# Four pairs by seven products, tiles at multiples of 64 bytes, and later transposes of the first hidden blocks in a four-layer float32 encoder

## The chip, the core and the metric

The kernel runs on one core of a Trainium2 chip. The metric is device time in microseconds (us) for one execution of the whole program. The engines are TensorE (PE, matmuls; its loads of the stationary operand are shown as PEld), VectorE (DVE), ScalarE (ACT), GpSimd (POOL) and SyncE (SP), which issues most DMAs. In the profile an operand name is a tile's name, and L229 is line 229 of the kernel.

## The reference, cut to what matters

The program computes four layers of an encoder on x of 256 rows and 1024 columns in float32. Each layer has a token mixer (chunked attention with a relative bias, gated linear attention, differential attention, and chunked attention again), a layer norm, a SwiGLU feed-forward with 2816 hidden columns, and a second layer norm:

```python
def swiglu(x, w_gate_up, w_down):
    g, u = jnp.split(x @ w_gate_up, 2, axis=-1)
    return (jax.nn.silu(g) * u) @ w_down

    for i in range(DEPTH):          # 4 layers
        y = mixer_i(h, ...)         # 0, 3: chunk band attention; 1: GLA; 2: differential attention
        h = layer_norm(DN_ALPHA * h + y, ln1_g[i], ln1_b[i])
        h = layer_norm(DN_ALPHA * h + swiglu(h, ffn_w_gate_up[i], ffn_w_down[i]), ln2_g[i], ln2_b[i])
```

## The kernel before

**Products.** Every float32 operand of a large product is split into a high part, rounded to the type fp32r, and a low part, the rest. A product is then three matmuls: high by high, low by high, high by low. `w_tiles` loads a pair of k-tiles of weights into `raw` (SP issues the DMA), casts the high part `wh` on ACT (L130) and subtracts the low part `wl` on DVE (L131). Two forms of product read these tiles. `run_rows` (L208 to L210) has activations as the stationary operand (`xT`, or `slab` in the output projections) and weights of 512 columns as the moving one. `run_cols` (L229, L230) has weights as the stationary operand and the activations as the moving one, 512 columns (both parts) and 256 columns (the high part): one pair of matmuls for each k-tile, eight pairs for each of the four blocks of a chunk, each block in one of four `mm` banks.

**The feed-forward** (`ffn`) runs over 11 chunks of 256 hidden columns, which are the 11 pairs of k-tiles of the down-projection. Chunks 0 and 1 go by rows: `row_done` makes the Silu on ACT (L932) and the product with the other half on DVE (L934), and `turn_hidden` transposes the result on PE (L943). Chunks 2 to 10 go by columns: `col_done` copies a block out of its bank on ACT (L968) and adds on DVE (L969). The hidden values are kept in `plain`, split into high and low.

**Seven products.** A pair in `SEVEN` is treated as a 2 by 2 product of blocks, which `seven_products` makes with 7 block products and not 8. Its hidden blocks go to `hid`; `combine` makes four sums of blocks on POOL (L916 to L919), and five steps later `split` makes the high parts on ACT (L924) and the low parts on DVE (L925), into `seven`. Its weights are loaded by `load`, which also makes three differences on DVE (L1015, into `tt` and back into `raw`) and then splits seven blocks and not four (`halves`: ACT L143, DVE L144). Each product of the down-projection is the three matmuls L1027 to L1029. After the last pair in `SEVEN`, `gather` adds the groups of products to the layer's sum on DVE. The loads of a chunk are written into the order one chunk ahead of its products; the tiles come from two rings, `raw` with 24 KB and `split` with 64 KB in each partition, in the pool `wp`.

**Order.** The code's order is the engines' order, except where a step is put off: `defer(n, f)` runs `f` after `n` steps of `tick`, one step for three matmuls of `run_rows`, for two pairs of `run_cols`, or for one product of the down-projection. `D_HIDDEN` is the number for `turn_hidden`, `D_COMBO` that for `split`.

**Addresses.** The pools lie one behind the other in each partition: `const` (`ident`, `powt`), `wp` (both rings), `act` (`h`, `xT`, the working tiles `k1`, small tiles), then the pool of the stage (`slab`, `k2`, `k3`, `plain`, `hid`, `seven`, `tt`, `gb`). A tile's size is rounded up to 32 bytes. `powt` holds 4 bytes and takes 32, so that in the built program all large tiles of `wp` and `act` start 32 bytes past a multiple of 64. The tiles of every stage start at a multiple of 64.

Of the kernel before, what the change touches and what calls it, by code (L numbers as in the profile page):

```python
# [9 lines left out]
F32 = mybir.dt.float32  # L10
# [5 lines left out]
P = 128  # L16
# [12 lines left out]

D_SCORES, D_TURN, D_TURN_DIFF, D_VALUES, D_VALUES_DIFF, D_OUT = 4, 7, 6, 3, 2, 6  # L30
D_GATE2, D_GATE3, D_STATE, D_READ, D_GLA_OUT = 3, 8, 2, 4, (6, 5)
D_NORM, D_HIDDEN, D_COMBO = 8, 4, 5
WARM = 24

SEVEN = (0, 3, 6)


@with_exitstack  # L40
def trunk_kernel(
# [27 lines left out]
    nc = tc.nc  # L69

    const = ctx.enter_context(tc.tile_pool(name="const", bufs=1))
# [3 lines left out]
    act = ctx.enter_context(tc.tile_pool(name="act", bufs=1))  # L75
# [18 lines left out]
    def st(shape, dtype, tag, bufs):  # L94
        return stage[-1].tile(shape, dtype, tag=tag, bufs=bufs, name=nm(tag))
# [18 lines left out]

    ident = const.tile([P, P], F32, tag="ident", name="ident")
    make_identity(nc, ident)
    powt = const.tile([P, 1], F32, tag="powt", name="powt")
    nc.gpsimd.memset(powt, -0.5)


    def w_tiles(chunk, s, fine=False):
# [17 lines left out]
    def halves(w, n):  # L139

        wh = split_ring.tile([P, n, 512], F32R, name=nm("wh"))
        wl = split_ring.tile([P, n, 512], F32R, name=nm("wl"))
        nc.scalar.copy(out=wh, in_=w)  # L143
        nc.vector.tensor_tensor(out=wl, in0=w, in1=wh.bitcast(F32), op=ALU.subtract)  # L144
        return [(wh[:, k, :], wl[:, k, :]) for k in range(n)]
# [95 lines left out]
    def put(dst, ks, cs, val):  # L241

        h = dst[:, ks, cs]
        nc.scalar.copy(out=h, in_=val)
        nc.vector.tensor_tensor(
            out=dst[:, ks, slice(256 + cs.start, 256 + cs.stop)],
            in0=val,
            in1=h.bitcast(F32),
            op=ALU.subtract,
        )  # L250
# [639 lines left out]
    def ffn(xT, layer, norm):  # L890
# [8 lines left out]
        n_pairs = FFN // 256  # L899
        rest = [c for c in range(n_pairs) if c not in SEVEN]  # L900
        plain = st([P, 2 * len(rest), 4 * P], F32R, "plain", 1)
# [20 lines left out]
        def split(c, f):  # L922
            x = seven[c] = st([P, 2, 7, P], F32R, "seven", len(SEVEN))
            nc.scalar.copy(out=x[:, 0], in_=f[:, 0:7, :])  # L924
            nc.vector.tensor_tensor(  # L925
                out=x[:, 1], in0=f[:, 0:7, :], in1=x[:, 0].bitcast(F32), op=ALU.subtract
            )
# [11 lines left out]
        def turn_hidden(c, t, hd):  # L939
            b = bank()  # L940
            for k in range(2):
                ks = slice(k * P, (k + 1) * P)
                nc.tensor.transpose(b[:, ks], hd[:, ks], ident)  # L943
            if c not in SEVEN:
                put(
# [17 lines left out]
        def col_done(c):  # L963
            g = {}

            def done(blk, b):
# [8 lines left out]
                gg = g.pop(k)  # L975
                if c not in SEVEN:
                    nc.vector.tensor_tensor(out=lo, in0=lo, in1=gg, op=ALU.mult)
# [26 lines left out]
        def load(c):  # L1004
            raw = raw_ring.tile([P, 4, 512], F32, name=nm("raw"))
            nc.sync.dma_start(raw, w_down[layer, c].rearrange("p (k n) -> p k n", k=4))
            if c not in SEVEN:
                parts[c] = halves(raw[:, 0:2], 2) + halves(raw[:, 2:4], 2)
# [39 lines left out]
        def seven_products(c):  # L1048
            for i, (a, b) in FORMS.items():
# [4 lines left out]
                    parts[c][b],  # L1054
                    c == SEVEN[-1] and i not in where,
                )
# [75 lines left out]
    for i in range(depth):  # L1132
# [18 lines left out]
        in_stage(ffn, norm1.xT, i, norm2)  # L1151
        xT = norm2.xT


def _layouts(inputs):

# [81 lines left out]
```

## Time and profile before

| | us |
|---|---|
| median of 3 runs | 1226.15 |
| lowest and highest run | 1224.26, 1227.82 |
| the profiled execution | 1226.83 |
| its span, first to last instruction | 1224.9 |
| PE busy | 1199.9 (98%) |
| DVE busy | 899.6 (73%) |
| ACT busy | 680.6 (56%) |
| POOL busy | 147.1 (12%) |

The profile is of one execution. A row of the timeline has a start, a duration, the engine, the line and the operation with its tiles, and in brackets how long the engine idled before it and what ended that. A matmul's printed duration overlaps with the next one's; the distance between two starts is what the queue pays. The granted clock of PE is at the upper of its two levels (1.2 and 2.4 GHz) all along.

### The profile page before, as it was taken

To read this page: it belongs to the slowest core of one execution; us is meant where nothing else is said; L and a number is where in the kernel's file an instruction comes from. 1 tells how busy PE (TensorE), PEld (TensorE's weight loads), DVE (VectorE), ACT (ScalarE), POOL (GpSimd) and SP (SyncE) were. 2 spreads that over 40 slices of the span, in tenths; PEclk is the share of its full clock that TensorE was granted. 3 is DMA by queue.
4 is the path that set the end of the run, shared out by engine and by line. 5 is a ranking of instruction groups with operands and counts; after the bars stand their busy time and mean duration, and the time that the engine had idled before them with its cause. 6 is when DMAs were issued, how large, how long until landed. Compare 5 with 4: busy or idle time off the path is not lost.

```text
span 1224.9 us, 17125 instructions
## 1 busy us (share of the span) xinstructions
PE 1199.9 (98%) x6212; PEld 990.0 (81%) x6212; DVE 899.6 (73%) x1490; ACT 680.6 (56%) x1185; POOL 147.1 (12%) x268
## 2 busy tenths in 40 slices
PE   8999999999999999999999999999999999999996
PEld 7888788888677878888887777888888888788885
DVE  6688766787656767677867786677786888676875
ACT  6566565653564455655446656566544774565550
POOL 1210101000211110110022211010002200101000
PEclk9999999999999999999999999999999999999999
DMA  9654645555474455556564355555656544655541
GB/s 362 213 181 125 213 157 194 190 194 202 144 230 132 139 188 197 179 181 227 194 211 153 127 162 171 202 190 176 218 189 232 188 139 147 198 171 199 189 172 35
DMA packets 56692, 223.88 MB, mean 183 GB/s; under 512 B 6816, under 2 KB 7328, under 8 KB 50976
## 3 DMA queue, kind: packets, MB, share of 16 engines
q1 hardware_dynamic: 51264, 206.59, 50.1%
q0 software_dynamic: 4768, 15.15, 3.9%
q10 hardware_dynamic: 576, 1.05, 0.3%
q8 instruction: 49, 0.80, 0.3%
q14 instruction: 35, 0.29, 0.1%
HBM read 221.71 MB, written 1.05 MB: 182 GB/s over the span
## 4 chain that ended last, share of the span: by engine, by line
PE 89%; POOL 3%; DVE 2%; DMA 2%; ACT 2%; issue 2%; POOLq 0%; DVEq 0%; ACTq 0%
PE mm L229 28%; PE mm L230 14%; PE mm L208 7%; PE mm L209 7%; PE mm L210 7%; PE tp L1027 5%; PE tp L1029 5%; PE tp L1028 5%; PE tp L468 2%; PE tp L257 1%; PE mm L1027 1%; PE mm L1028 1%; PE mm L1029 1%; PE tp L537 1%; DMA k<-in_c_bias_dram 1%
## 5 line engine op out<-in xcount | busy, mean ns | idle before, releaser
L229 PE MATMUL mm<-xT,wh 128*128 128x512 f32 x1568 | 559.3, 400 | 0.0
L230 PE MATMUL mm<-xT,wl 128*128 128x256 f32 x1568 | 441.4, 281 | 0.0
L131 DVE TENSOR_TENSOR wl<-raw,wh 128x1024 fp32r<-128x1024 f32 (+1 forms) x306 | 369.4, 1216 | 63.9 <-ACT wh L130 61.6
L130 ACT CAST wh<-raw 128x1024 fp32r<-128x1024 f32 (+1 forms) x306 | 314.0, 1045 | 112.6 <-PE mm L209 58.9
L229 PEld LDWEIGHTS mm<-xT,wh 128*128 128x128 f32 x1568 | 294.8, 188 | 74.3 <-issue 4.6
L230 PEld LDWEIGHTS mm<-xT,wl 128*128 128x128 f32 x1568 | 296.5, 189 | 0.7 <-issue 0.3
L144 DVE TENSOR_TENSOR wl<-raw,wh 128x1024 fp32r<-128x1024 f32 (+1 forms) x88 | 105.0, 1220 | 22.9 <-PE tp L1029 11.8
L208 PE MATMUL mm<-wh,xT 128*128 128x512 f32 x304 | 120.1, 398 | 1.6 <-ACT wh L130 1.3
L210 PE MATMUL mm<-wl,xT 128*128 128x512 f32 x304 | 119.4, 393 | 0.6 <-DVE wl L131 0.5
L209 PE MATMUL mm<-wh,xT 128*128 128x512 f32 x304 | 119.5, 394 | 0.0
L143 ACT CAST wh<-raw 128x1024 fp32r<-128x1024 f32 (+2 forms) x88 | 90.4, 1050 | 43.3 <-PE tp L1027 22.6
L969 DVE TENSOR_TENSOR k<-mm,k 128x256 f32<-128x256 f32 x144 | 60.5, 420 | 60.5 <-ACT k L968 60.5
L1027 PE MATMUL tp<-wl,plain 128*128 128x512 f32 x256 | 102.0, 398 | 0.0
L1028 PE MATMUL tp<-wh,plain 128*128 128x512 f32 x256 | 101.5, 396 | 0.0
L1029 PE MATMUL tp<-wh,plain 128*128 128x512 f32 x256 | 101.4, 396 | 0.0
L968 ACT COPY k<-mm 128x256 f32<-128x256 f32 x144 | 53.4, 370 | 62.2 <-PE mm L230 61.9
L208 PEld LDWEIGHTS mm<-wh,xT 128*128 128x128 f32 x304 | 56.9, 188 | 15.9 <-ACT wh L130 2.3
L209 PEld LDWEIGHTS mm<-wh,xT 128*128 128x128 f32 x304 | 57.1, 188 | 13.4 <-issue 1.2
L210 PEld LDWEIGHTS mm<-wl,xT 128*128 128x128 f32 x304 | 57.1, 188 | 13.3 <-DVE wl L131 1.8
L1029 PEld LDWEIGHTS tp<-wh,plain 128*128 128x128 f32 x256 | 48.2, 188 | 11.8
L282 POOL TENSOR_SCALAR sm<-mv 128x1 f32<-128x1 f32 x16 | 11.9, 746 | 380.6 <-DVE mv L346 380.6
L1028 PEld LDWEIGHTS tp<-wh,plain 128*128 128x128 f32 x256 | 48.2, 188 | 11.5
(190 smaller groups left out, 1478.4 us busy)
## 6 DMA issues: line engine op xcount, KB each, us to landing
raw<-in_w_gu_dram SPq DMA_DIRECT2D x176, 512.0 KB, 4.3
raw<-in_w_down_dram SPq DMA_DIRECT2D x44, 1024.0 KB, 5.0
raw<-in_a_qkv_dram SPq DMA_DIRECT2D x46, 512.0 KB, 5.3
raw<-in_b_in_dram SPq DMA_DIRECT2D x24, 512.0 KB, 4.3
raw<-in_c_qkv_dram SPq DMA_DIRECT2D x24, 512.0 KB, 4.4
raw<-in_a_o_dram SPq DMA_DIRECT2D x16, 512.0 KB, 3.8
k<-in_a_bias_dram POOLq DMA_DIRECT2D x16, 256.0 KB, 4.7
raw<-in_b_o_dram SPq DMA_DIRECT2D x8, 512.0 KB, 4.0
```

Source lines behind the costliest of these rows:

```text
L130: nc.scalar.copy(out=wh[:, k, :], in_=raw[:, k, :])
L131: nc.vector.tensor_tensor(out=wl[:, k, :], in0=raw[:, k, :], in1=wh[:, k, :].bitcast(F32), op=ALU.subtract,)
L143: nc.scalar.copy(out=wh, in_=w)
L144: nc.vector.tensor_tensor(out=wl, in0=w, in1=wh.bitcast(F32), op=ALU.subtract)
L208: nc.tensor.matmul(b, xh, wh, start=first, stop=False)
L209: nc.tensor.matmul(b, xl, wh, start=False, stop=False)
L210: nc.tensor.matmul(b, xh, wl, start=False, stop=last)
L229: nc.tensor.matmul(b, wh[:, cs], xk, start=kt == 0, stop=False)
L230: nc.tensor.matmul(b[:, :256], wl[:, cs], xk[:, :256], start=False, stop=kt == NKT - 1)
L1027: nc.tensor.matmul(o, xh, wl, start=start, stop=False)
L1028: nc.tensor.matmul(o, xh, wh, start=False, stop=False)
L1029: nc.tensor.matmul(o, xl, wh, start=False, stop=stop)
```

## The change

Three numbers change, and two tiles. `SEVEN` has pairs 0, 2, 4 and 6 in place of 0, 3 and 6, so that `plain` has 14 rows and not 16, `seven` has four buffers and not three, and one plain pair lies between two pairs by seven. `D_HIDDEN` goes from 4 to 10 steps. `powt` becomes the first column of a tile of 32 columns (128 bytes), and a tile of 32 bytes is added at the end of `act`; in the built program all large tiles then start at a multiple of 64 bytes.

```diff
-D_NORM, D_HIDDEN, D_COMBO = 8, 4, 5
+D_NORM, D_HIDDEN, D_COMBO = 8, 10, 5
-SEVEN = (0, 3, 6)
+SEVEN = (0, 2, 4, 6)
-    powt = const.tile([P, 1], F32, tag="powt", name="powt")
-    nc.gpsimd.memset(powt, -0.5)
+    pad = const.tile([P, 32], F32, tag="powt", name="powt")
+    nc.gpsimd.memset(pad, -0.5)
+    powt = pad[:, 0:1]
...
         in_stage(ffn, norm1.xT, i, norm2)
         xT = norm2.xT
+    act.tile([P, 8], F32, tag="pad", bufs=1, name="pad")
```

In the changed file lines after L118 stand two lines lower: L932 is L934 there, L943 is L945, L1015 is L1017.

ScalarE, first layer, where the row products of chunks 0 and 1 end and the column products begin. `hid_1441` and `hid_1466` are pair 0's blocks, `k_341` and `k_339` are the Silu of chunk 1's second half. Before:

```order
L130 CAST wh_1673<-raw_1672 128x1024
L959 COPY hid_1441<-tp_1518 128x128
L960 COPY hid_1441<-tp_1518 128x128
L130 CAST wh_1679<-raw_1678 128x1024
L924 CAST seven_1546<-hid_1441 128x896
L932 ACTIVATE k_341_1542<-mm_1508 128x256
L130 CAST wh_1685<-raw_1684 128x1024
L244 CAST plain_1348<-tp_1586 128x2x128
L968 COPY k_359_1595<-mm_1573 128x256
```

Now:

```order
L132 CAST wh_1686<-raw_1685 128x1024
L934 ACTIVATE k_339_1533<-mm_1503 128x256
L961 COPY hid_1466<-tp_1566 128x128
L962 COPY hid_1466<-tp_1566 128x128
L926 CAST seven_1600<-hid_1466 128x896
L970 COPY k_357_1587<-mm_1561 128x256
L973 ACTIVATE k_357_1587<-k_357_1587 128x256
L970 COPY k_360_1611<-mm_1591 128x256
L246 CAST plain_1348<-tp_1621 128x2x128
```

The Silu moved ahead of pair 0's copies and cast; behind the cast there are now the copies of the first column blocks.

TensorE at the same place: the transposes of chunk 1's second half (`k_342` before, `k_340` now) among the column products of chunk 2. Before, in the first block:

```order
L230 MATMUL mm_1573<-xT_1276,wl_1563 128x256
L943 MATMUL tp_1586<-ident,k_342_1544 128x128 x2
L229 MATMUL mm_1573<-xT_1276,wh_1568 128x512
L230 MATMUL mm_1573<-xT_1276,wl_1569 128x256
L229 MATMUL mm_1573<-xT_1276,wh_1568 128x512
```

Now, in the third block:

```order
L231 MATMUL mm_1616<-xT_1276,wh_1538 128x512
L232 MATMUL mm_1616<-xT_1276,wl_1539 128x256
L945 MATMUL tp_1621<-ident,k_340_1535 128x128 x2
L231 MATMUL mm_1616<-xT_1276,wh_1544 128x512
L232 MATMUL mm_1616<-xT_1276,wl_1545 128x256
```

They moved from behind 12 column matmuls to behind 36.

VectorE, first layer, where the last column chunks end and the loads of the down-projection begin; `raw_2600` and `raw_2604` are pair 1, `raw_2638` and `raw_2642` pair 2. Before:

```order
L245 TENSOR_TENSOR plain_1348<-k_513_2458,plain_1348 128x256
L969 TENSOR_TENSOR k_530_2529<-mm_2512,k_530_2529 128x256
L977 TENSOR_TENSOR k_530_2529<-k_530_2529,k_528_2508 128x256
L245 TENSOR_TENSOR plain_1348<-k_530_2529,plain_1348 128x256
L969 TENSOR_TENSOR k_532_2552<-mm_2535,k_532_2552 128x256
L144 TENSOR_TENSOR wl_2603<-raw_2600,wh_2602 128x1024
L144 TENSOR_TENSOR wl_2607<-raw_2600,wh_2606 128x1024
L144 TENSOR_TENSOR wl_2641<-raw_2638,wh_2640 128x1024
```

Now:

```order
L1017 TENSOR_TENSOR tt_2644<-raw_2642 128x1024
L247 TENSOR_TENSOR plain_1348<-k_516_2462,plain_1348 128x256
L971 TENSOR_TENSOR k_533_2533<-mm_2516,k_533_2533 128x256
L1017 TENSOR_TENSOR tt_2644<-tt_2644,raw_2642 128x512
L979 TENSOR_TENSOR k_533_2533<-k_533_2533,k_531_2512 128x256
L1017 TENSOR_TENSOR raw_2642<-raw_2642,tt_2644 128x512
L247 TENSOR_TENSOR plain_1348<-k_533_2533,plain_1348 128x256
L971 TENSOR_TENSOR k_535_2556<-mm_2539,k_535_2556 128x256
L146 TENSOR_TENSOR wl_2607<-raw_2604,wh_2606 128x1024
L146 TENSOR_TENSOR wl_2611<-raw_2604,wh_2610 128x1024
L146 TENSOR_TENSOR wl_2646<-raw_2642,wh_2645 128x512
L146 TENSOR_TENSOR wl_2652<-tt_2644,wh_2651 128x1536
```

Pair 2, now one by seven, has its three differences between the last sums of the column chunks, ahead of pair 1's subtractions.

## Rows read from the trace of the kernel before

**Rows 1.** The page: busy time of each engine, granted clock, chain by engine.
```profile
PE 1199.9 (98%) x6212; PEld 990.0 (81%) x6212; DVE 899.6 (73%) x1490; ACT 680.6 (56%) x1185; POOL 147.1 (12%) x268
...
PEclk9999999999999999999999999999999999999999
...
PE 89%; POOL 3%; DVE 2%; DMA 2%; ACT 2%; issue 2%; POOLq 0%; DVEq 0%; ACTq 0%
```

**Rows 2.** PE's waits: who waited for whom, total us, times, longest us.
```profile
PE tp L943 <- DVE k L934: 6.1, 4, 1.6
PE tp L624 <- DVE k L611: 1.5, 2, 0.8
```

**Rows 3.** Timeline at one of the four waits (start, duration, engine, operation, idle before).
```profile
146.42 0.46 POOL L919 TENSOR_TENSOR hid<-hid 128x128 f32<-128x128 f32 x1
146.91 0.94 ACT L924 CAST seven<-hid 128x896 fp32r<-128x896 f32 x1 [2.40 <-POOL hid L919]
147.76 0.38 ACT L932 ACTIVATE k<-mm 128x256 f32<-128x256 f32 x1
148.17 0.42 DVE L934 TENSOR_TENSOR k<-k,mm 128x256 f32<-128x256 f32 x1 [2.15 <-ACT k L932]
148.65 0.44 PE L943 MATMUL tp<-ident,k 128*128 128x128 f32 x2 [1.51 <-DVE k L934]
```

**Rows 4.** PE's timeline, columns: first and last of 39 pairs.
```profile
195.20 0.40 PE L229 MATMUL mm<-xT,wh 128*128 128x512 f32 x1
...
208.98 0.40 PE L229 MATMUL mm<-xT,wh 128*128 128x512 f32 x1
```

**Rows 5.** PE's timeline, down-projection: two starts with 48 distances between them.
```profile
269.67 0.40 PE L1027 MATMUL tp<-wl,plain 128*128 128x512 f32 x1
...
280.92 0.39 PE L1027 MATMUL mm<-wl,seven 128*128 128x512 f32 x1
```

**Rows 6.** DVE's timeline, down-projection: pair 6's load, and the last loads.
```profile
265.02 1.83 DVE L144 TENSOR_TENSOR wl<-raw,wh 128x1024 fp32r<-128x1024 f32 x2 [0.19 <-PE tp L1029]
266.77 1.22 DVE L1015 TENSOR_TENSOR tt<-raw 128x1024 f32<-128x1024 f32 x1
...
270.33 1.76 DVE L144 TENSOR_TENSOR wl<-tt,wh 128x1536 fp32r<-128x1536 f32 x1 [0.89 <-ACT wh L143]
272.01 1.75 DVE L144 TENSOR_TENSOR wl<-raw,wh 128x1536 fp32r<-128x1536 f32 x1
...
279.77 1.23 DVE L144 TENSOR_TENSOR wl<-raw,wh 128x1024 fp32r<-128x1024 f32 x1 [2.98 <-PE tp L1029]
...
288.99 3.49 DVE L144 TENSOR_TENSOR wl<-raw,wh 128x1024 fp32r<-128x1024 f32 x3
```

**Rows 7.** Groups by line and shape: busy us, mean ns of one, idle before.
```profile
L144 DVE TENSOR_TENSOR wl<-raw,wh 128x1024 fp32r<-128x1024 f32 x64 | 76.4, 1221 | 22.3 <-PE tp L1029 11.8 <-ACT wh L143 6.5 <-issue 4.0
```

**Rows 8.** ACT's waits: the cast of `split` for POOL.
```profile
ACT seven L924 <- POOL hid L919: 29.2, 12, 2.4
```

**Rows 9.** PE's timeline, output projection, stationary `slab`: first and last of 47 distances.
```profile
107.13 0.39 PE L208 MATMUL mm<-wh,slab 128*128 128x512 f32 x1
...
118.13 0.40 PE L210 MATMUL mm<-wl,slab 128*128 128x512 f32 x1
```

**Rows 10.** PE's timeline, rows, stationary `xT`: first and last of 32 distances.
```profile
23.45 0.39 PE L208 MATMUL mm<-wh,xT 128*128 128x512 f32 x1
...
30.70 0.39 PE L210 MATMUL mm<-wl,xT 128*128 128x512 f32 x1
```

**Rows 11.** Groups by line and shape, DVE (columns as in rows 7).
```profile
L131 DVE TENSOR_TENSOR wl<-raw,wh 128x1024 fp32r<-128x1024 f32 x302 | 366.7, 1223 | 62.6 <-ACT wh L130 60.3
L925 DVE TENSOR_TENSOR seven<-hid,seven 128x896 fp32r<-128x896 f32 x12 | 13.1, 1092 | 16.6 <-ACT seven L924 16.6
```

**Rows 12.** PE's timeline: first and fourth matmul of a run in `values2`.
```profile
48.53 0.40 PE L558 MATMUL tp<-k,slab 128*128 128x512 f32 x1
...
49.23 0.27 PE L558 MATMUL tp<-k,slab 128*128 128x256 f32 x1
```

## The prediction

> **What bounds the kernel now.** I read the page first. TensorE (PE) is busy for 1199.9 of 1224.9 us, and its granted clock is at the upper level in every slice [rows 1]; PE also carries 89% of the chain that ended last [rows 1]. So a change is worth what it takes from PE's own queue, or from PE's waits. Next I read PE's waits: they are small, and the largest is one line, the transposes of the first hidden blocks (L943), which wait 6.1 us in four pieces, one per layer [rows 2]. Last I read PE's timeline for the distance between starts of matmuls that follow each other without a wait. The duration printed for a matmul (0.39 us) overlaps with the next; what PE pays is the distance.
>
> **Term 1, the first transposes put off.** The timeline at one of the four waits shows how it comes [rows 3]. GpSimd (POOL) ends its four sums for pair 0 at 146.88. Until then the cast of `split` (L924) holds ScalarE (ACT) for 2.40 us, and the Silu of chunk 1's second half (L932) stands behind that cast. VectorE's product (L934) follows, and L943 starts on PE at 148.65 after 1.51 us of idling. In the new order this Silu stands ahead of the cast, and the transposes come ten steps of the order after their product and not four. So the whole wait goes: 6.1 us. What covers it now: between the end of the row products and the transpose PE has 36 column matmuls, 18 pairs of 0.353 us [rows 4] = 6.4 us, against the 1.3 us or so that Silu, product and their gaps take (147.76 to 148.65) [rows 3]. If that cover failed, the price would be the 1.5 us again, in each layer [rows 2]. What is late next: the cast of pair 0 now holds ACT while the copies of the first column blocks (L968) queue behind it. POOL's sums and the cast last about 4 us, they begin after some 0.7 us of column products, and the first block ends after 8 x 0.353 = 2.8 us. Its copy thus comes some 3 to 4 us late. PE needs that bank back only for its fifth block, after 4 x 2.8 = 11.3 us, since there are four `mm` banks. I cost this at nothing; the rival on ACT below is the case in which it isn't.
>
> **Term 2, a fourth pair by seven products.** A plain pair takes 8 products and a pair by seven takes 7, each of 3 matmuls of 512 columns. That is 3 matmuls fewer a layer, 12 in all. In the down-projection 48 of them take 280.92 - 269.67 = 11.25 us [rows 5], 0.234 us each, so 2.8 us go. PE's share is certain, since the instructions are gone. What it adds lies on other engines. VectorE's work for such a load runs from 266.2 to 273.8 (the h11 part, three differences, two subtractions of 1536 columns, and 0.89 us of waiting for ACT) [rows 6]: about 7.6 us, against 2 x 1.22 = 2.4 us for a plain one [rows 7]. A pair by seven and a plain one together ask 10.0 us of VectorE, while PE works on the two for 45 matmuls, 10.5 us at today's distance. Today VectorE runs ahead and waits for room in the ring (2.98 us) [rows 6], and the load that ended at 273.8 is used at 280.92: a lead of 7 us. With the new pattern the lead no longer grows, but the order also starts pair 2's differences inside the last column chunks, where VectorE idles. The last loads end at 292.48 [rows 6], after the sums of the seven groups; their order against those sums changes by one row only. So I cost it at nothing, with an upper bound of 1.5 us a layer: that is by how much VectorE would miss PE's last loads if its lead at the start of the phase were lost. On ACT and POOL there are 16 waits of this kind and not 12 [rows 8]; the ones that stand inside the column chunks cost PE nothing today, since PE's waits name none for them [rows 2].
>
> **Term 3, the tiles' start addresses.** Before, everything in `wp` and `act` starts 32 bytes past a multiple of 64, and the stage's tiles at a multiple of 64; afterwards all large tiles start at a multiple. The trace shows what this can be worth. The same code (L208 to L210), with the same moving tiles from the ring, takes 47 distances in 118.13 - 107.13 = 11.00 us where the stationary tile is `slab` [rows 9], 0.234 us each, but 32 distances in 30.70 - 23.45 = 7.25 us where it is `xT` [rows 10], 0.2266 us each. The first two tiles start 32 bytes apart modulo 64, the second two alike. The down-projection (`plain`, `seven` against the ring) is of the first kind and shows the first distance [rows 5]. I take the equal start as what counts: after the change all of these are alike. That gives 1008 matmuls of the down-projection x (0.2344 - 0.2266) = 7.9 us and 384 of the output projections x 0.0074 = 2.8 us, 10.7 us together; as after an interruption the first few keep the longer distance, I take 10.0. On columns (L229 and L230) and rows on `xT` the two tiles start alike before and after, so I take no change there. VectorE shows none: L131, all of it 32 past, takes 1223 ns for 1024 columns and L925, all of it at multiples, 1092 ns for 896, 1.02 ns for each column between [rows 11].
>
> The bounds of this term: both operands at multiples of 64 occur in one place, L558 to L560, three matmuls of 512 columns in a row. They take 49.23 - 48.53 = 0.70 us, 0.233 each [rows 12], which is near the longer distance; but three matmuls after a change of operands are too few to settle. So at worst the down-projections gain nothing, and the 912 row matmuls on `xT` rise from 0.2266 to 0.2344: +7.1 us. At best the columns gain as well: 512 + 256 columns at the granted 2.4 GHz are 0.320 us, and with the 13 ns per matmul by which the rows on `xT` exceed their 0.2133 [rows 10] a pair is 0.3467 in place of 13.78 / 39 = 0.3533 [rows 4]: 1568 x 0.0066 = -10.4 us.
>
> A rule speaks against this term. The Trainium skill, "SBUF — State Buffer", sections Specifications (TRN2) and Who interferes with whom, has lines of 16 bytes, so that a start at 32 is as good as one at 64, and gives PE two independent read ports, one for the moving and one for the stationary operand. By it the two distances should not differ [rows 9, 10], term 3 would be zero and the sum 1217.9, the first rival's time; they differ by 3%, so the measurement decides.
>
> **The sum**, against the profiled execution's own 1226.83 us: - 6.1 - 2.8 - 10.0 = 1207.9. The median of the runs is 0.7 us below that execution; I say **1207.5**.
>
> **Rivals.**
> - *The start addresses do nothing* (the distance on `slab` comes from something else, such as where the tiles lie in the ring). The short run at multiples of 64 speaks for it [rows 12], the two distances against it [rows 9, 10]. 1226.83 - 6.1 - 2.8 = 1217.9.
> - *Columns gain too*: 1207.9 - 10.4 = 1197.5. For it: on columns a matmul exceeds its 2.4 GHz time by 17 ns on average [rows 4], more than on rows [rows 10]; against it: their two tiles start alike already.
> - *All matmuls go near the clock's own time.* If a start at a multiple of 64 removed all but 2.5 ns of the excess, 512 columns would take 0.2158 and 256 columns 0.1092 us: the rows on `xT` gain 912 x 0.0108 = 9.8, the other 512-column ones 1392 x 0.0184 = 25.6, the pairs 1568 x 0.0283 = 44.4 us, and the time is 1138. The 0.23 at multiples of 64 speaks against it [rows 12]. (The Trainium skill, "TensorE: Matmul & The Clock Gate", section Back-to-back issue gap, has that N/2.4 + 2.5 ns; no stretch of this trace comes near it.)
> - *Rows get worse*: the worst end of term 3, 1217.9 + 7.1 = 1225.0.
> - *VectorE becomes the bound of the down-projection*: with PE at 0.2266 the 45 matmuls take 10.2 us against VectorE's 10.0, so that any lost lead stays lost. The lead of 7 us speaks against it [rows 6]. Up to 4 x 1.5: 1213.9.
> - *Slower: every `split` holds PE as the first one does today.* Now 16 casts wait on ACT for POOL. If what stands behind each (a Silu or a copy of a column block, a cast of weights) were wanted by PE within those 2.4 us, PE would lose 1.5 us sixteen times and not four: 1226.83 + 12 x 1.5 - 2.8 - 10.0 = 1232. It decides where four banks and the loaded chunk don't cover the cast; that PE waits at none of the eight casts inside the columns speaks against it [rows 2, 8].
> - *The change doesn't do what it says*: left out, since the built program has 12 matmuls less and the starts named above.
>
> **Chances.** The forecast 0.48; addresses do nothing 0.19; columns gain too 0.13; near the clock's time 0.03; VectorE binds 0.08; rows worse 0.05; slower 0.04. A measurement of this kernel can tell some 0.3%, 3.7 us, from no change, so only the case of worse rows counts as the same: faster 0.91, same 0.05, slower 0.04. The range takes in the forecast, the columns' gain and the idle addresses with the spread of the runs: 1196 to 1219.
>
> **What would show it.** Term 1: no wait of PE for L934 among PE's waits, and the Silu ahead of the cast in ACT's timeline. Term 2: 1008 products' matmuls in the down-projection and no wait of PE for VectorE's `wl` there; if VectorE binds, such a wait appears in the last third of the phase. Term 3: distances of 0.227 us on `slab`, `plain` and `seven`. If these stay at 0.234, the addresses do nothing; if the columns' pair leaves 0.353, they do more than I gave them; if rows on `xT` leave 0.2266 upwards, the worst end holds. My forecast is wrong above all if the equal start is not what separates the two distances [rows 9, 10].

## The result and the profile after

The changed kernel takes 1212.28 us in the median of four runs (1211.46 to 1214.09), the kernel before 1226.99 beside it: a ratio of 0.9886, 95% interval 0.9865 to 0.9907. I had said 1207.5, and 1196 to 1219. So the direction and the range held, and about three quarters of the gain came (13.9 of 18.9 us, by the profiled executions); but the parts of the sum didn't come as I had put them. The profiled execution took 1212.91 us, 13.9 less than that of before.

The page of the changed kernel: busy time of each engine, the granted clock in 40 slices, the chain by engine (beside [rows 1]).

```profile
PE 1193.0 (98%) x6200; PEld 989.5 (82%) x6200; DVE 913.0 (75%) x1502; ACT 682.7 (56%) x1185; POOL 153.7 (13%) x284
...
PEclk9999999999899999999999999999999999999998
...
PE 89%; DVE 4%; DMA 2%; ACT 2%; POOL 2%; issue 1%; POOLq 0%; DVEq 0%; ACTq 0%
```

The twelve matmuls are gone, and PE is still the engine to look at. New is the 8 in the clock's eleventh slice (the 8 in the last slice lies behind PE's last matmul). PE's waits, as in [rows 2] (total us, times, longest):

```profile
PE tp L736 <- DMA k<-in_b_b_g_dram: 2.5, 1, 2.5
...
PE tp L626 <- DVE k L613: 0.9, 2, 0.7
...
PE mm L1029 <- DVE k L971: 0.6, 1, 0.6
```

The wait of 6.1 us at the hidden blocks' transposes (L945 now) is gone. A wait for a DMA in gated linear attention (gla) has grown from 1.5 to 2.5 us, and a small one for VectorE has come in a down-projection. Before, the wait in gla was:

```profile
PE tp L734 <- DMA k<-in_b_b_g_dram: 1.5, 1, 1.5
```

I then took PE's timeline apart by stretches, each from its first start to its last end:

| us | before | after | difference |
|---|---|---|---|
| columns of the four feed-forwards | 415.5 | 403.9 | -11.6 |
| four down-projections | 242.4 | 238.6 | -3.8 |
| first row products of gla | 34.8 | 37.7 | +2.9 |
| output projections | 109.0 | 108.3 | -0.7 |
| all else | | | -0.7 |

The waits of 1.5 us lay in the columns and explain 6.1 of the 11.6. The other 5.5 are columns that come faster, which my forecast didn't have. Column pairs, timeline of PE, each time two starts with 39 pairs between them as in [rows 4]; first layer, then last layer:

```profile
179.69 0.39 PE L231 MATMUL mm<-xT,wh 128*128 128x512 f32 x1
...
193.21 0.39 PE L231 MATMUL mm<-xT,wh 128*128 128x512 f32 x1
...
1074.62 0.40 PE L231 MATMUL mm<-xT,wh 128*128 128x512 f32 x1
...
1088.40 0.40 PE L231 MATMUL mm<-xT,wh 128*128 128x512 f32 x1
```

In the first layer 39 pairs take 13.52 us, 0.3467 each; in the last one 13.78, 0.3533, which is what all layers took before. Layers two and three are as the first. Pair by pair, the fast stretch repeats one distance for hundreds of pairs, and the slow one repeats a cycle of three pairs of 1.060 us together. The two patterns begin at the last transposes (L945) and last to the end of the phase; in the first layer the 16 pairs just ahead of these transposes still take 0.3527 each, in the last layer 0.3469, so that the switch happens there.

The down-projection and the output projection, two starts with 48 and with 47 distances between them, beside [rows 5] and [rows 9]:

```profile
259.62 0.39 PE L1031 MATMUL tp<-wh,seven 128*128 128x512 f32 x1
...
270.77 0.39 PE L1031 MATMUL tp<-wh,seven 128*128 128x512 f32 x1
...
107.16 0.39 PE L210 MATMUL mm<-wh,slab 128*128 128x512 f32 x1
...
118.07 0.40 PE L212 MATMUL mm<-wl,slab 128*128 128x512 f32 x1
```

That is 11.15 / 48 = 0.2323 and 10.91 / 47 = 0.2321 us: shorter than 0.2344 and 0.2340, but not the 0.2266 of the forecast.

The first transposes, first layer (start, duration, engine, operation, idle before), beside [rows 3]:

```profile
145.79 0.37 ACT L934 ACTIVATE k<-mm 128x256 f32<-128x256 f32 x1
...
147.06 0.41 DVE L936 TENSOR_TENSOR k<-k,mm 128x256 f32<-128x256 f32 x1
...
148.51 0.46 POOL L921 TENSOR_TENSOR hid<-hid 128x128 f32<-128x128 f32 x1
...
149.00 0.94 ACT L926 CAST seven<-hid 128x896 fp32r<-128x896 f32 x1 [2.52 <-POOL hid L921]
...
151.39 0.38 PE L945 MATMUL tp<-ident,k 128*128 128x128 f32 x2
```

The cast still holds ACT, for 2.52 us, but the Silu is done ahead of it, the product follows at 147.06, and the transposes come at 151.39 without a wait. The copies of the column blocks that now queue behind the cast cost PE nothing: the four banks cover them.

What was lost, in gla (the same columns):

```profile
312.56 2.35 DVE L133 TENSOR_TENSOR wl<-raw,wh 128x1024 fp32r<-128x1024 f32 x2
314.83 0.28 DVE L688 TENSOR_TENSOR k<-k,k 128x128 fp32r<-128x128 f32 x1
...
312.97 2.29 POOL L667 TENSOR_SCALAR_AFFINE_SELECT k<-k 128x128 f32<-128x128 f32 x1
...
317.05 0.48 POOL L698 DMA_DIRECT2D k<-in_b_b_g_dram  x1
...
319.90 2.04 PE L736 MATMUL tp<-k,k 65*128 65x512 f32 x2 [2.54 <-DMA k<-in_b_b_g_dram]
```

And the same place before:

```profile
317.05 1.22 DVE L131 TENSOR_TENSOR wl<-raw,wh 128x1024 fp32r<-128x1024 f32 x1
318.19 0.29 DVE L686 TENSOR_TENSOR k<-k,k 128x128 fp32r<-128x128 f32 x1
...
317.49 1.14 POOL L665 TENSOR_SCALAR_AFFINE_SELECT k<-k 128x128 f32<-128x128 f32 x1
```

POOL's `affine_select` starts while VectorE subtracts and ends 0.15 us after the last of VectorE's subtractions there, a small one of the gate's weights (L688, before L686). Now two subtractions of `raw` stand ahead of the small one and `affine_select` takes 2.29 us; before, one stood there and it took 1.14. The load of the gate's weights is issued behind it on POOL, and PE waits for that load. Behind the wait, the granted clock (each row: the window, its length, PE busy with its count, then the clock):

```profile
318.00:322.00 4.00, 2.10 (x4) 0.68 0.14 54
322.00:326.00 4.00, 4.00 (x14) 0.50 0.00 0
```

The clock is at the lower of its two levels, 1.2 GHz, for most of these 8 us, and row products there start 0.427 us apart in place of 0.227. Before, it stayed at the upper level all along.

### The profile page after: what moved, and what is told of

It reads as the page before. It is cut to its first block, busy times and chain, and to the rows that moved or that the text cites. A ratio compares the mean times of both kernels' runs of the same rounds, so it can differ in the third digit from the quotient of the medians.

```text
span 1211.2 us, 17131 instructions
## 1 busy us (share of the span) xinstructions
PE 1193.0 (98%) x6200; PEld 989.5 (82%) x6200; DVE 913.0 (75%) x1502; ACT 682.7 (56%) x1185; POOL 153.7 (13%) x284
## 4 chain that ended last, share of the span: by engine, by line
PE 89%; DVE 4%; DMA 2%; ACT 2%; POOL 2%; issue 1%; POOLq 0%; DVEq 0%; ACTq 0%
PE mm L231 26%; PE mm L232 13%; PE mm L210 8%; PE mm L211 8%; PE mm L212 8%; PE tp L1029 5%; PE tp L1030 5%; PE tp L1031 5%; PE tp L470 2%; PE mm L1029 1%; PE mm L1031 1%; PE mm L1030 1%; PE tp L259 1%; DVE wl L133 1%; PE tp L539 1%
## 5 line engine op out<-in xcount | busy, mean ns | idle before, releaser
L133 DVE TENSOR_TENSOR wl<-raw,wh 128x1024 fp32r<-128x1024 f32 (+1 forms) x306 | 368.1, 1211 | 61.8 <-ACT wh L132 58.6
L146 DVE TENSOR_TENSOR wl<-raw,wh 128x1024 fp32r<-128x1024 f32 (+2 forms) x88 | 104.4, 1218 | 12.7 <-ACT wh L145 9.0
L1029 PE MATMUL tp<-wl,plain 128*128 128x512 f32 x224 | 88.9, 397 | 0.0
L1030 PE MATMUL tp<-wh,plain 128*128 128x512 f32 x224 | 88.4, 395 | 0.0
L1031 PE MATMUL tp<-wh,plain 128*128 128x512 f32 x224 | 88.4, 395 | 0.0
L971 DVE TENSOR_TENSOR k<-mm,k 128x256 f32<-128x256 f32 x144 | 60.3, 419 | 36.6 <-ACT k L970 36.5
L210 PE MATMUL mm<-wh,slab 128*128 128x512 f32 x128 | 51.5, 404 | 0.0
L211 PE MATMUL mm<-wh,slab 128*128 128x512 f32 x128 | 51.1, 399 | 0.0
```

Of the source, the lines that this page charges most:

```text
L133: nc.vector.tensor_tensor(out=wl[:, k, :], in0=raw[:, k, :], in1=wh[:, k, :].bitcast(F32), op=ALU.subtract,)
L210: nc.tensor.matmul(b, xh, wh, start=first, stop=False)
L211: nc.tensor.matmul(b, xl, wh, start=False, stop=False)
L1029: nc.tensor.matmul(o, xh, wl, start=start, stop=False)
L1030: nc.tensor.matmul(o, xh, wh, start=False, stop=False)
L1031: nc.tensor.matmul(o, xl, wh, start=False, stop=stop)
```

## Experiments

Three theories stood at the start. A: the start addresses set the distance between matmuls, and the columns gained by them as well. B: the distance follows a repeating pattern which an interruption of the stream sets, so that the columns' gain came from where the transposes stand; addresses do nothing. C, later: the idle time of 1.5 us put the columns into the slow pattern.

**The transposes alone.**

```diff
-D_NORM, D_HIDDEN, D_COMBO = 8, 4, 5
+D_NORM, D_HIDDEN, D_COMBO = 8, 10, 5
```

> The kernel before with D_HIDDEN 10 in place of 4, and nothing else. Theory A (start addresses set the distance between matmuls): only the four waits at L943 go, 6.1 us, so about 1220.9; the column phase of a feed-forward falls from 103.9 to 102.4 us and its pairs stay at 0.353 us. Theory B (the distances follow a repeating pattern that an interruption of the stream sets; addresses don't matter): with the transposes at another place the pairs fall to 0.347 us in some layers, column phase 100.6 us there, and the time goes as low as 1213.6 if all four layers do.

1214.45 us, a ratio of 0.9902 (0.9888 to 0.9915): 12.65 less than before, with the old addresses. Column phases are 100.5 us in all four layers. Columns of the first layer, 39 pairs apart:

```profile
179.82 0.28 PE L230 MATMUL mm<-xT,wl 128*128 128x256 f32 x1
...
193.34 0.28 PE L230 MATMUL mm<-xT,wl 128*128 128x256 f32 x1
```

13.52 us, the fast pattern. So most of the whole change is this one number: 6.1 us of waiting and some 7 us of columns.

**The addresses alone.** The edit is that of the changed kernel, on the kernel before:

```diff
-    powt = const.tile([P, 1], F32, tag="powt", name="powt")
+    pad = const.tile([P, 32], F32, tag="powt", name="powt")
...
+    act.tile([P, 8], F32, tag="pad", bufs=1, name="pad")
```

> The kernel before with the addresses of the changed kernel (powt in a tile of 128 bytes, the tile of 32 bytes at the end of act), and nothing else. Theory A: down-projections and output projections gain 1.7 ns for each matmul as in the changed kernel, 2.3 us, and the columns of the feed-forward up to 1.8 us a layer, so 1217.5 to 1224.7; the four waits of 1.5 us at L943 stay. Theory B: no difference that can be measured, 1227, pairs at 0.353 and the down-projection at 0.234 us.

1225.63 us against 1227.10, a ratio of 0.9992 (0.9983 to 1.0001): the time alone can't tell this from nothing. The timeline can. The down-projection, 48 distances:

```profile
259.83 0.39 PE L1031 MATMUL tp<-wh,plain 128*128 128x512 f32 x1
...
270.99 0.39 PE L1031 MATMUL tp<-wh,plain 128*128 128x512 f32 x1
```

11.16 us, 0.2325 each as in the changed kernel, and each down-projection takes 60.35 us in place of 60.81. The columns of the feed-forwards stay at 0.3533 in all layers, and the wait stays:

```profile
PE tp L945 <- DVE k L936: 6.1, 4, 1.5
```

So A holds for the down-projection and the output projections, with some 2.5 us, and B for the feed-forwards' columns.

**Four pairs by seven alone.**

```diff
-SEVEN = (0, 3, 6)
+SEVEN = (0, 2, 4, 6)
```

> The kernel before with SEVEN = (0, 2, 4, 6), and nothing else. Twelve matmuls fewer at 0.234 us: 2.8 us, 1224.2, by both theories; each down-projection falls from 60.81 to 60.1 us and the four waits at L943 stay. Rival (VectorE binds the down-projection): waits of PE for wl there, up to 1.5 us a layer, and up to 1230.

1225.02 us, a ratio of 0.9987 (0.9978 to 0.9995). The down-projections fall from 60.81 to 60.06 us, three matmuls each as expected, and PE waits for no `wl` there. But the first row products of gla take 36.6 us and not 34.8, since the wait for the gate's weights is there already:

```profile
PE tp L734 <- DMA k<-in_b_b_g_dram: 2.8, 1, 2.8
```

POOL's `affine_select` takes 2.29 us in this kernel too, and 1.14 in the two above, which have three pairs by seven. In the profiled execution the fourth pair by seven thus gives back more than half of its 2.8 us in the next stage.

**All but the addresses.**

> The changed kernel with the addresses of the kernel before (powt 4 bytes, no tile at the end of act). Theory A: without the addresses' gain, 1226.99 - 6.1 - 2.8 = 1218.1, and up to 1221 if the GLA stage falls to the lower clock for some us as in the changed kernel; pairs of columns at 0.353, down-projection at 0.234 us. Theory B: as the changed kernel, about 1212.3, with most feed-forward columns at 0.347 us.

1213.96 us, a ratio of 0.9894 (0.9881 to 0.9908), 1.7 us above the changed kernel, a difference that the two intervals don't tell from none. Columns of the first layer:

```profile
179.61 0.39 PE L229 MATMUL mm<-xT,wh 128*128 128x512 f32 x1
...
193.13 0.39 PE L229 MATMUL mm<-xT,wh 128*128 128x512 f32 x1
```

Fast in all four layers, without the new addresses. The changed kernel differs by the addresses alone, and its last layer is slow, so together with the other edits the addresses take part in what picks a layer's pattern. The 1.7 us lost there are about what they gain in the down- and output projections. In gla PE waits 2.9 us and the clock falls.

**Another place for the transposes.**

```diff
-D_NORM, D_HIDDEN, D_COMBO = 8, 4, 5
+D_NORM, D_HIDDEN, D_COMBO = 8, 7, 5
```

> The kernel before with D_HIDDEN 7: the Silu stands ahead of the cast as with 10, but the transposes interrupt the columns only once, behind 24 matmuls. The wait of 6.1 us goes: 1221.0 by all theories if the pairs of columns stay at 0.353 us. Theory B (an interruption sets the pattern): each layer falls into one of the patterns seen, 0.353 or 0.347 us, so column phases of 102.4 or 100.6 us and 1213.6 to 1221.0. Theory C (the idle time of 1.5 us itself puts the columns into the slow pattern): without it all four layers are at 0.347, 1213.6.

1216.51 us, a ratio of 0.9908 (0.9895 to 0.9922). No wait at L943 is left, but the layers differ: column phases of 100.3, 102.1, 100.3 and 102.1 us. Columns of the first layer, then of the second:

```profile
179.78 0.28 PE L230 MATMUL mm<-xT,wl 128*128 128x256 f32 x1
...
193.30 0.28 PE L230 MATMUL mm<-xT,wl 128*128 128x256 f32 x1
...
479.75 0.40 PE L229 MATMUL mm<-xT,wh 128*128 128x512 f32 x1
...
493.53 0.40 PE L229 MATMUL mm<-xT,wh 128*128 128x512 f32 x1
```

13.52 and 13.78 us. Theory C falls as it stood: two layers are slow without any wait ahead. Theory B's mix is what came.

**Which difference of the addresses counts.** The changed kernel's tiles all start at multiples of 64, but `slab`, `plain` and `seven` at 128 modulo 256, the ring at 0. Four kernels move the stage's tiles alone, by the size of the tile at the end of `act`; the fourth has the ring and `xT` where the kernel before had them. The first:

```diff
-    act.tile([P, 8], F32, tag="pad", bufs=1, name="pad")
+    act.tile([P, 40], F32, tag="pad", bufs=1, name="pad")
```

> The changed kernel with the stage's tiles moved up by 128 bytes, so that all large tiles start at a multiple of 256 and not only of 64. If an equal start modulo 256 is what the rows on xT have and slab, plain and seven lack, their distance falls from 0.2326 to 0.228 us: 1008 x 4.6 + 384 x 4.4 ns = 6.3 us, 1206. If only a multiple of 64 counts, the distance stays at 0.2326 and the time at 1212.

1208.33 us, one run. The down-projection, 48 distances:

```profile
259.74 0.39 PE L1031 MATMUL mm<-wh,seven 128*128 128x512 f32 x1
...
270.62 0.39 PE L1031 MATMUL tp<-wh,seven 128*128 128x512 f32 x1
```

10.88 us, 0.2267 each: the distance that I had forecast. Down-projections take 232.4 us together and not 238.6; one layer's columns fell into the slow pattern, 1.7 us.

Without the tile at the end of `act` (the stage at 96 modulo 256, the ring at 0):

> The changed kernel without the tile at the end of act: the stage's tiles start 32 bytes past a multiple of 64, the ring, h and xT stay at a multiple. If what counts is that both tiles of a matmul start alike, slab, plain and seven go back to 0.234 us, 2.4 us more than the changed kernel, 1214.7. If what counts is the ring's own start, they stay at 0.2326 and the time at 1212.

1214.86 us, one run, and 0.2342 us:

```profile
259.75 0.39 PE L1029 MATMUL tp<-wl,seven 128*128 128x512 f32 x1
...
270.99 0.40 PE L1029 MATMUL tp<-wl,plain 128*128 128x512 f32 x1
```

With 24 columns in place of 8 (the stage at 192, the ring at 0):

> The changed kernel with the stage's tiles 64 bytes higher: they start at 192 modulo 256, the ring, h and xT at 0, so all still at multiples of 64. If the difference of the two starts modulo 256 sets the distance, slab, plain and seven are not at 0.227 us but at 0.2326 or 0.2343, 1212 to 1215. If a common start modulo 64 or 128 were enough in some other way, they would fall to 0.227 as in e5_mod256, 1207.

1212.39 us, one run. I had given it the distances seen so far; it has one of its own, 10.99 / 48 = 0.2290 us:

```profile
259.71 0.39 PE L1029 MATMUL mm<-wl,seven 128*128 128x512 f32 x1
...
270.70 0.39 PE L1029 MATMUL tp<-wl,seven 128*128 128x512 f32 x1
```

And the kernel without the new addresses, with only a tile of 40 columns at the end of `act`, so that ring, `xT` and stage all start at 160 modulo 256, none at a multiple of 64:

> The kernel of e4_no_addr (the ring, h and xT at 160 modulo 256, 32 bytes past a multiple of 64) with the stage's tiles moved up by 160 bytes, so that all large tiles start at 160 modulo 256 and none at a multiple of 64. If an equal start counts and not the multiple, slab, plain and seven fall from 0.2342 to 0.227 us: 1213.96 - 1008 x 7.2 ns - 384 x 6 ns = 1204.4, or up to 1212 if columns leave the fast pattern in all layers. If the multiple of 64 counts, the distance stays at 0.2342 and the time at 1214.

1206.36 us, a ratio of 0.9836 (0.9819 to 0.9852), 7.6 less than the same kernel without that tile (0.9894), from one line:

```profile
259.71 0.39 PE L1027 MATMUL tp<-wl,seven 128*128 128x512 f32 x1
...
270.59 0.39 PE L1027 MATMUL tp<-wl,seven 128*128 128x512 f32 x1
```

10.88 us again. So of these two an equal start is what counts, not the multiple of 64:

| stage less ring, modulo 256 | kernels | distance, us |
|---|---|---|
| 0 | e5_mod256, e11_equal32 | 0.2267 |
| 192 | e10_diff64 | 0.2290 |
| 128 | changed kernel, e2_addr | 0.2323 to 0.2325 |
| 96 | kernel before, e6_stage32 | 0.2342 to 0.2344 |

That 256 and not a larger number is the period isn't shown; these are the differences that were tried. The Trainium skill, "SBUF — State Buffer", Specifications (TRN2) and Who interferes with whom, would have them all alike, by its lines of 16 bytes and two independent read ports of PE; the table differs by 3%, and the measurement decides.

**The gate's loads ahead.** In `gla` the memset and the three loads of the gate's weights go ahead of POOL's constants, in the changed kernel:

```diff
-        cst = k2([P, 512])
...
         g1 = k1([P, NKT, 16])
...
         nc.gpsimd.dma_start(g2[64:65, :], b_g.unsqueeze(0))
+        cst = k2([P, 512])
...
+        nc.gpsimd.affine_select(
```

> The changed kernel with the loads of the gate's weights (b_w_g2, b_b_g) and their memset ahead of POOL's constants in gla. If PE's wait of 2.5 us at L736 and the half clock behind it come from the load being issued behind POOL's affine_select, both go: the first row products of gla fall from 37.7 to 33.3 us (the 34.8 of before less its wait of 1.5), and the time to 1208. Rival (the half clock comes from something else, such as the power of the faster stream): the wait goes, the half clock stays, 1210.

1208.54 us, a ratio of 0.9849 (0.9828 to 0.9870), 3.7 less than the changed kernel. The wait for the DMA is gone. POOL's `affine_select` comes later, meets only the last 0.14 us of a subtraction, and takes 0.29 us:

```profile
314.02 1.22 DVE L133 TENSOR_TENSOR wl<-raw,wh 128x1024 fp32r<-128x1024 f32 x1
...
315.09 0.29 POOL L685 TENSOR_SCALAR_AFFINE_SELECT k<-k 128x128 f32<-128x128 f32 x1
```

The row products of gla take 35.1 us and not the 33.3 expected, since in the profiled execution the clock still fell, a little later and behind a wait of 1.0 us for VectorE (L745):

```profile
322.00:326.00 4.00, 3.02 (x15) 1.00 0.00 0
326.00:330.00 4.00, 4.00 (x19) 0.61 0.69 202
```

**Both together**, the tile of 40 columns (e5_mod256) and the gate's loads ahead (e7_gla), on the changed kernel:

> The changed kernel with both: the stage's tiles at a multiple of 256 (e5_mod256) and the gate's loads ahead of POOL's constants (e7_gla). If the two gains add, 1212.3 - 3.9 (1008 x 5.6 ns and 384 x 4 ns would be 7.2, less what one layer's columns lost in e5_mod256) - 3.7: 1203 to 1205. If the shorter distance in the down-projection makes a VectorE load late, a wait of PE for wl shows there and the time stays above 1207.

1203.53 us, a ratio of 0.9815 (0.9800 to 0.9830): the gains add, and this beats both kernels. The row products of gla take 33.7 us with the clock up throughout, the down-projection stays at 0.2267, and PE waits for no `wl` there.

**The changed kernel once more.**

> The changed kernel once more, unchanged. If the pattern of a layer's columns is fixed by the program, the first three layers' column phases are again 100.55 us and the last one's 102.27. If small differences in arrival decide, at least one layer differs by 1.7 us, and the time of single runs spreads by that much, 1210 to 1214.

1215.70 us, one run. The column phases are 100.55, 100.55, 100.55 and 102.27 us, to 0.01 the same as in the first profile; in these two executions the program fixed the pattern of a layer. The last layer's columns:

```profile
1074.63 0.40 PE L231 MATMUL mm<-xT,wh 128*128 128x512 f32 x1
...
1088.41 0.40 PE L231 MATMUL mm<-xT,wh 128*128 128x512 f32 x1
```

The spread of single runs comes from elsewhere: here PE waited 3.6 us for the gate's weights and 2.4 for L613, against 2.5 and 0.9. The load of the gate's weights took 3.75 us from its issue to its landing here and 2.72 in the first profile, so that the first row products of gla took 38.7 us and not 37.7.

## Why the prediction was right or wrong

**Term 1 was right in what it claimed, and too small.** The wait of 6.1 us went, the cover held, and the copies behind the cast cost nothing. (Two readings were off, without touching the sum: from the Silu's start to the transposes [rows 3] has 0.9 us and not 1.3, and by my own numbers, 0.7 + 4 - 2.8, the first block's copy comes some 2 us late and not 3 to 4.) What I missed is that a transpose in a stream of matmuls also sets how the matmuls behind it follow each other. I moved the transposes on paper and kept the pair at 0.353 us. The runs: 0.3467 in all layers of e1_hidden, in two of e8_hidden7, in three of the changed kernel, there 5.5 us. The rows for this were in the trace: some column stretches before already ran at the shorter distance (in gla 31 pairs from 343.88 to 354.63, 0.3468 each), but I had looked at the mean of the feed-forward alone.

**The rival "columns gain too" had the number and not the cause.** I gave it a pair of 0.3467, which is what came, and put it down to the addresses. The addresses alone leave 0.3533 in the feed-forwards (e2_addr), and with the later transposes all four layers run at 0.3467 without them (e1_hidden, e4_no_addr).

**Term 2 was right on PE and wrong on its cover.** Twelve matmuls went, 2.8 us, and each down-projection kept VectorE ahead, but for one wait of 0.55 us in the third layer, where the sum that frees a bank stood behind two subtractions:

```profile
842.79 2.48 DVE L146 TENSOR_TENSOR wl<-raw,wh 128x1024 fp32r<-128x1024 f32 x2 [0.42 <-ACT wh L145]
...
845.19 0.42 DVE L971 TENSOR_TENSOR k<-mm,k 128x256 f32<-128x256 f32 x1
```

That is the rival on VectorE, in one layer of four and at a third of its price. The step that failed in this term is "I cost it at nothing": I followed ACT and POOL through the columns and stopped at the end of the down-projection. With the fourth pair, VectorE has two subtractions of weights together where POOL makes its constants for gla; POOL's `affine_select` is held up by them, the load behind it comes later, PE waits, and the clock may fall. Price: 1.8 us (e3_seven, where the clock stayed up), 2.9 in the changed kernel's first profile and 3.9 in its second (e12_again). Two steps show the cause: the fourth pair alone brings the 2.29 us in place of 1.14 and the longer wait (e3_seven), and with the loads issued ahead of the `affine_select` the wait is gone (e7_gla). The Trainium skill, "SBUF — State Buffer", section SBUF: two separate sides, has VectorE and GpSimd share one pair of ports as an exclusive lock, in which the other blocks fully; the trace agrees, with the end of POOL's `affine_select` 0.15 us behind that of the last subtraction that it meets, beside one, beside two, and where it meets only the last 0.14 us of one.

**Term 3 had the right mechanism and the wrong period.** I wrote that I take the equal start as what counts, and read "equal" modulo 64. The rows could not tell that: [rows 9] had a difference of 96 modulo 256, [rows 10] of 0, and the change made it 128. In place of 10.0 us it gave about 1008 x 1.8 + 384 x 1.7 ns = 2.5. Where the start is made equal modulo 256, the forecast distance comes (e5_mod256, e11_equal32: 7.6 us). The rows on `xT` kept their distance, as forecast (a mean of 0.228 before and after). [rows 12], the short run at multiples of 64, tells nothing either way: both of its tiles lie in the stage's pool, so that they start alike modulo 256 in every kernel here, and as the first three behind an interruption they still take 0.71 us in e5_mod256, where long runs are at 0.2267 each.

**The sum.** Against the profiled execution: 1226.83 - 6.1 (waits) - 5.5 (columns) - 2.8 (matmuls) - 2.5 (addresses) + 2.9 (gla) + 0.6 (VectorE) = 1213.4, measured 1212.91. That the forecast time was near is luck: a gain that I hadn't seen (5.5 us of columns) stood in for most of one that I had put too high (the addresses, 2.5 us and not 10.0), and the loss in gla was not in the sum at all. The cases were split wrongly too: "addresses do nothing" and "columns gain too" both came in part, together.

## What to carry to other kernels

Where one engine is the bound, list the distance between its starts for each stretch, pair by pair and not as a mean: two values of the same code are a gain that an edit elsewhere can switch on or off. When tiles meet in one matmul, look at the difference of their start addresses modulo 256; a tile of some bytes moves it (here it also moved one layer's columns into the slow pattern, for 1.7 us, in e5_mod256). And follow added work past the end of its own stage, on every engine that shares something with it: here VectorE's subtractions held up POOL, and POOL's queue a load that PE wanted.

## What was not expected of the hardware

- PE's stream of 512 and 256 columns settles into one of several repeating patterns, 0.3467 or 0.3533 us a pair, and keeps it until something else stands in the stream; the changed kernel repeated it in a second execution, layer by layer. What picks the pattern at an interruption stays open.
- The start-to-start distance of a 512-column matmul was 0.2267, 0.2290, 0.2323 or 0.2343 us, by the difference of its two tiles' start addresses.
- The clock fell to 1.2 GHz behind an idle time of 2.5 us in gla (the changed kernel), but not behind 2.8 us there (e3_seven), and once behind 1.0 us (e7_gla), where the same wait of 1.0 us left it up in e9_both. What decides it was not tried.
- A 128x128 `affine_select` on POOL that starts while VectorE subtracts ended 0.15 us behind the last of these subtractions, after 0.29, 1.14 or 2.29 us. The DMAs behind it in POOL's order came after it.
